# Two-layer hybrid diffusion backbone: three sums of the first layer's conditioning matrix are formed in another stage, four row tiles at a time

## The chip, the core and the metric

The kernel runs on one core of a Trainium2 chip. The metric is the device time of one execution in microseconds; the times before are three runs with a median of 1243.5 us. All other numbers come from one profiled execution of the kernel before. TensorE is written PE, VectorE DVE, ScalarE ACT, GpSimd POOL, and SP is the engine whose queue issues most DMAs.

## The reference, cut to what matters

There are two layers. The first one is attention beside a Fourier mix, both fed by one input projection and joined by one output projection; then a gated convolution FFN. Each layer takes six vectors (two shifts, two scales, two gates) from the conditioning vector c:

```python
def ada_params(cond, w_ada_i, b_ada_i):
    m = jax.nn.silu(cond) @ w_ada_i + b_ada_i          # (1024,) @ (1024, 6*1024)
    ...
    return jnp.split(m, 6, axis=-1)

sh1, sc1, g1, sh2, sc2, g2 = ada_params(c, w_ada[i], b_ada[i])
h_lat = modulate(rmsnorm(x_lat, g_mix[i]), sh1, sc1)
o_lat, o_ctx = hybrid_mixer(h_lat, h_ctx, w_in_hyb[j], ...)     # attention | Fourier, then @ w_out
x_lat = x_lat + g1 * o_lat
h = modulate(rmsnorm(x_lat, g_ffn[i]), sh2, sc2)
x_lat = x_lat + g2 * conv_ffn(h, w_up[i], w_fdw[i], b_fdw[i], w_down[i])
```

The change concerns three of these sums in the first layer: g1 (number 2), sh2 (number 3) and sc2 (number 4). g1 is needed when the output projection is added to x, sh2 and sc2 when the input of the FFN is formed behind it.

## The kernel before

The sequence has 512 rows, so four row blocks of 128. A product in the accurate format is three matmuls of 128x512 (mm3, lines 223 to 225), since each operand is split into a high part (a cast on ACT) and a low part (a subtraction on DVE). Weights arrive as chunks of 512 KB in tiles `st`, are split into `whi` (ACT, L195) and `wlo` (DVE, L196), and five chunks are held at a time.

The mixer runs in this order: input projection of q and kv; then `heads_and_fourier` (projection of the Fourier columns `project(t)`, normalised and rotated heads `k_T`, `q_T`, the transform over time `over_time(t)` with the table `dft`, the transform over channels `over_channels(ct)` with the table `cs`); then `attention`; then `token_major("wo")`, the output projection in two halves.

One sum of w_ada is formed from eight row tiles (`kt`) of 128x1024. For each of them there are two matmuls with cT (128x32) as weights and 512 columns (L338), which write 32 of the 128 rows of one PSUM bank each; the row tile's number, even or odd, and the column half choose which 32, so that two successive row tiles fill four different strips of the array. The trace shows each such fp32 matmul as two records, hence four records for one row tile. `columns` then copies the bank (L344), transposes it in four pieces (L347) and adds strips (L352, L353); `col` adds the bias (L360). `in_every_row` makes the gate a row for all partitions (eight matmuls, L369, and two copies, L370).

Sums 2 and 3 are a filler of `heads_and_fourier`: `fill` stands between its steps, and takes two row tiles at a time from the shared tiles `sa`, of which there are three. Sum 4 is a filler of the output projection: its eight row tiles are loaded into eight tiles `wn` of the pool `xs`, which is opened behind the attention.

Attention works on eight units (a row block and one of two kv heads), with four heads in a unit. For each head there are scores (four matmuls into one of two wide PSUM tiles `D`, L807), a maximum (DVE, L809), an exponential (ACT, L812), a reciprocal (DVE, L814) and a product (POOL, L815). For each unit there are six times four transposes (L824) into a bank `B`, a split of that bank into `pt` (ACT L290, DVE L291) and two matmuls with the values (L829). The scores of a unit are written ahead of the values of the unit before. There are four banks `B`.

The order on each engine is fixed when the program is built, by a scheduler that moves independent instructions past each other by its own estimate of times; every engine then works its list in that order, and the SP queue its own.

Of the kernel before, what the change touches and what calls it, by code (L numbers as in the profile page):

```python
# [17 lines left out]
P = 128  # L18
D = 1024
# [209 lines left out]
def tile_hybrid_backbone(ctx: ExitStack, tc: tile.TileContext, x_in, ctx_in, vecs_in, gains_in, cond_in, condT_in, wada, wnat,  # L229
# [40 lines left out]
    def pad(pool, nbytes):  # L270

        t = pool.tile([P, nbytes // 4], F32, tag="pad", name=nm("pad"), bufs=1)
        nc.gpsimd.memset(t, 0.0)

    pad(const, 32)
    pad(tp, 64)

    def vec(name, i=0, n=1):
        o = VEC[name] + i
        return vecs[:, o : o + n]  # L280
# [31 lines left out]
    def chunk_tile():  # L312
        return wp.tile([P, D], F32, tag="sa", name=nm("sa"), bufs=3)

    class Columns:
# [4 lines left out]
        def __init__(self, pool, row, nbuf):  # L320
            self.pool, self.row, self.nbuf = pool, row, nbuf
            self.st, self.g = [], None

        def load(self, n):
            for _ in range(n):
                if self.pool is None:
                    t = chunk_tile()
                else:
                    t = self.pool.tile([P, D], F32, tag="wn", name=nm("wn"), bufs=self.nbuf)
                nc.sync.dma_start(t, wnat[self.row + len(self.st)])  # L330
                self.st.append(t)
# [21 lines left out]
                nc.vector.tensor_tensor(out=raw[:, s], in0=v[:, s, :, 1, 0:2], in1=part[:, s], op=ALU.add)  # L353
            return raw

        def col(self, j):

            raw = self.columns()
            col = tiny(8)
            nc.vector.tensor_tensor(out=col.rearrange("p (s k) -> p s k", s=2), in0=raw[:, :, :, 0],  # L360
                                    in1=vec("ba", j * KT, KT).rearrange("p (s k) -> p s k", s=2), op=ALU.add)
# [49 lines left out]
    def run(gen, n=1):  # L411
        for _ in range(n):
            if next(gen, "end") == "end":
                return

    def drain(gen):
        for _ in gen:
            pass
# [229 lines left out]
    def heads_and_fourier(q_ps, kv_ps, rot, kgain, qT, kk, vv, four, sums):  # L648
        dft = [four.tile([P, TT, SEQ], F32R, tag=f"dft{i}", name=f"dft{i}") for i in range(2)]
        cs = four.tile([P, 2, 2, P], F32R, tag="cs", name="cs")  # L650
        for i in range(2):
# [92 lines left out]
            nc.vector.tensor_tensor(out=o[:, 257:512][:, ::-1], in0=X[:, 1:256], in1=ys[:, 1:256], op=ALU.add)  # L744
            split(*hsl(h, 4 + ct, 0, SEQ), o)

        def fills():
            for j, use in sums:
                group = Columns(None, j * KT, 0)
                group.load(3)  # L750
                for kt in range(KT):
                    if kt % 2 == 0:
                        yield
                    group.product(kt)
                    if kt + 3 < KT:
                        group.load(1)
                yield
                use(group.col(j))

        filler = fills()  # L760

        def fill():
            run(filler)

        project(0)
        kl = k_rows(0, TT)
        kc = k_rows(TT, NKEY)
# [6 lines left out]
        project(2)  # L774
        q_T(qr, 1)
        qr = [q_rows(2), q_rows(3)]
        fill()
        over_time(0)
        fill()
        over_time(1)  # L780
        fill()
        project(3)
        fill()
        q_T(qr[0], 2)
        q_T(qr[1], 3)
        fill()
        over_time(2)
        fill()
        over_time(3)
        fill()  # L790
        for ct in range(4):
            over_channels(ct)
            fill()
        drain(filler)
    
    def attention(qT, kk, vv, ap, fill):
        units = [(t, kv) for t in range(TT) for kv in range(NKV)]
# [51 lines left out]
    def token_major(key, kts, gate, fin, filler, n_fill):  # L849

        def part(t, kt, w, acc, n):
            mm3(nc, acc, hsl(h, kt, t * P, (t + 1) * P), tuple(u[:, (kt % 2) * 512 : (kt % 2 + 1) * 512] for u in w), n == 0, n == len(kts) - 1)

        D0, D1 = bank2(), bank2()
        acc = [D0[:, 0:512], D0[:, 512:1024], D1[:, 0:512], D1[:, 512:1024]]
        for n, kt in enumerate(kts):
            w = stream.get((key, 0, kt // 2))
            for t in range(TT):
                part(t, kt, w, acc[t], n)
            if n % 2 == 1:  # L860
                stream.release((key, 0, kt // 2))
            run(filler, n_fill)
        drain(filler)
        for t in range(TT):
            residual(t, 0, acc[t], gate)
        for t in range(TT):
            b = bank()
            for n, kt in enumerate(kts):
                part(t, kt, stream.get((key, 1, kt // 2)), b, n)
            residual(t, 1, b, gate)  # L870
            if t == TT - 1:
                for kt in kts[1::2]:
                    stream.release((key, 1, kt // 2))
            fin(t)

    def mixer():
        A2, S2 = mods[0]
        with ExitStack() as tables:
            keep = tables.enter_context(sbuf("keep", "right"))
            gain = keep.tile([P, 2, HD], F32, tag="gain", name="gain")  # L880
            with sbuf("pre") as pre:
                q_ps, kv_ps, rot = load_and_project(gain, keep, pre)
            with sbuf("qkv") as qkv:
                qT = qkv.tile([P, NQ, SEQ], F32R, tag="qT", name="qT")
                kk = [qkv.tile([P, NKV, SEQ + CTX], F32R, tag=f"kk{i}", name=f"kk{i}") for i in range(2)]
                vv = qkv.tile([P, NKEY, NKV, 2, HD], F32R, tag="vv", name="vv")
                with sbuf("four") as four:
                    heads_and_fourier(q_ps, kv_ps, rot, gain[:, 1, :], qT, kk, vv, four, [(2, lambda col: in_every_row(col, gate1)), (3, lambda col: in_rows(col, S2))])
                tables.close()
                with sbuf("att") as ap:  # L890
                    ahead = iter((0, 0, 1, 1, 1, 1, 1, 0))
                    attention(qT, kk, vv, ap, lambda: stream.fill(stream.loaded + next(ahead)))
        with sbuf("xs") as xp:
            group = Columns(xp, 4 * KT, KT)
            group.load(KT)

            def steps():
                for kt in range(KT):
                    yield
                    group.product(kt)  # L900
                in_rows(group.col(4), A2, "gf0")

            token_major("wo", (4, 5, 6, 7, 0, 1, 2, 3), gate1, finisher(xp, A2, S2), steps(), 1)


    def ffn(l, filler, filler1, mods, out_dram=None):
# [382 lines left out]
```

## Time and profile before

| | us |
|---|---|
| median of 3 runs | 1243.5 |
| lowest, highest | 1242.24, 1245.1 |
| the profiled execution's own time | 1242.08 |
| its span, first to last instruction | 1240.3 |
| PE busy in the span | 1172.2 (95%) |
| DVE busy | 764.1 (62%) |
| ACT busy | 588.1 (47%) |
| POOL busy | 260.3 (21%) |
| mean granted PE clock | 0.981 |

The profile's stages are read from the instructions' lines: the Fourier part runs to about 143 us, the attention to about 244 us (with parts of the output projection in its last 27 us), the output projection's remaining part to about 280 us, then the FFN begins. Busy shares are averages over stages with different limits; for the change the stretch from 108 to 258 us matters.

### The profile page before, as it was taken

Reading aid. Unit: us, or ns where it says so; the run is one execution under the profiler, and the core shown is the slowest. Engines: PE = TensorE matmul, PEld = TensorE weight load, DVE = VectorE, ACT = ScalarE, POOL = GpSimd, SP = SyncE. Lnnn points to the kernel's source line nnn. Section 1 sums busy time; section 2 is a strip of 40 time slices with the busy share of each in tenths; the row PEclk is TensorE's granted clock in tenths of the full one; section 3 lists DMA queues with packets and bytes.
Section 4 is the critical chain, followed back from the end, with each engine's and each line's share of the span. In section 5 each row is a group of like instructions: output and inputs, shape, how many; then the busy total and the mean of one; then the engine's idle time right before and its main releaser. Section 6 shows DMA issues by size and latency. Waiting matters only on the chain.

```text
span 1240.3 us, 15425 instructions
## 1 busy us (share of the span) xinstructions
PE 1172.2 (95%) x5813; PEld 962.7 (78%) x5813; DVE 764.1 (62%) x1092; ACT 588.1 (47%) x1021; POOL 260.3 (21%) x164
## 2 busy tenths in 40 slices
PE   4899899999996999999999999979999999999998
PEld 1686477769885888888888877868988888888886
DVE  3458599346987667554646675664686545555563
ACT  4454587325766664334444543342574433433441
POOL 2025255001677830000001650000250000000000
PEclk8999999999998999999999998989999999999999
DMA  9534600222666653222234443101264232232230
GB/s 361 219 135 160 204 1 1 99 105 86 244 224 238 228 206 133 100 89 101 86 102 154 156 139 105 55 17 51 86 207 132 85 103 88 99 102 92 95 119 34
DMA packets 43834, 156.43 MB, mean 126 GB/s; under 512 B 5008, under 2 KB 5520, under 8 KB 43504
## 3 DMA queue, kind: packets, MB, share of 16 engines
q1 hardware_dynamic: 42192, 149.51, 34.9%
q0 software_dynamic: 1120, 5.54, 1.3%
q8 instruction: 46, 0.75, 0.2%
q10 hardware_dynamic: 448, 0.39, 0.1%
q14 instruction: 28, 0.23, 0.1%
HBM read 153.33 MB, written 2.10 MB: 125 GB/s over the span
## 4 chain that ended last, share of the span: by engine, by line
PE 73%; DVE 10%; DMA 7%; ACT 4%; issue 3%; POOL 2%; SPq 0%; POOLq 0%; ACTq 0%; DVEq 0%
PE B L223 17%; PE B L224 16%; PE B L225 16%; PE D L223 6%; PE D L224 6%; PE D L225 6%; DVE wlo L196 3%; DMA sa<-in_wada_dram 3%; DMA st<-in_wall_dram 2%; POOL sa L384 2%; PE B L829 2%; PE B L338 1%; DMA wn<-in_wnat_dram 1%; DVE tiny L809 1%; ACT P L812 1%
## 5 line engine op out<-in xcount | busy, mean ns | idle before, releaser
L196 DVE TENSOR_TENSOR wlo<-st,whi 128x1024 fp32r<-128x1024 f32 x174 | 239.2, 1378 | 245.0 <-ACT whi L195 242.0
L223 PE MATMUL B<-h,whi 128*128 128x512 f32 (+1 forms) x880 | 313.8, 370 | 10.9 <-DVE tmp L925 8.8
L224 PE MATMUL B<-h,whi 128*128 128x512 f32 (+1 forms) x880 | 321.8, 369 | 0.0
L225 PE MATMUL B<-h,wlo 128*128 128x512 f32 (+1 forms) x880 | 320.3, 368 | 0.0
L195 ACT CAST whi<-st 128x1024 fp32r<-128x1024 f32 x174 | 182.1, 1049 | 177.2 <-PE B L224 101.7
L223 PEld LDWEIGHTS B<-h,whi 128*128 128x128 f32 x880 | 162.3, 190 | 39.2 <-issue 9.4
L224 PEld LDWEIGHTS B<-h,whi 128*128 128x128 f32 x880 | 167.2, 190 | 26.8
L225 PEld LDWEIGHTS B<-h,wlo 128*128 128x128 f32 x880 | 166.8, 190 | 27.1
L384 POOL TENSOR_TENSOR sa<-sa,scb 128x1024 f32<-128x1024 f32 x56 | 153.9, 2767 | 79.1 <-DMA sa<-in_wada_dram 39.1
L290 ACT CAST g<-g 128x512 fp32r<-128x512 f32 x88 | 54.6, 621 | 153.6 <-DVE g L933 74.4
L287 POOL TENSOR_TENSOR tiny<-tiny,mhalf 128x1 f32<-128x1 f32 (+3 forms) x26 | 21.2, 816 | 462.4 <-DVE tiny L286 461.2
L291 DVE TENSOR_TENSOR g<-g,g 128x512 fp32r<-128x512 f32 x88 | 69.9, 795 | 71.4 <-ACT g L290 71.4
L387 ACT ACTIVATE sa<-sa 128x512 f32<-128x512 f32 x112 | 69.5, 624 | 30.3 <-POOL sa L384 30.1
L224 PE MATMUL D<-wlo,g 128*128 128x512 f32 x176 | 68.5, 389 | 0.0
L225 PE MATMUL D<-whi,g 128*128 128x512 f32 x176 | 68.5, 389 | 0.0
L223 PE MATMUL D<-whi,g 128*128 128x512 f32 x176 | 68.5, 389 | 0.0
L223 PE MATMUL B<-whi,g 128*128 128x512 f32 x176 | 68.5, 389 | 0.0
L224 PE MATMUL B<-wlo,g 128*128 128x512 f32 x176 | 68.5, 389 | 0.0
L225 PE MATMUL B<-whi,g 128*128 128x512 f32 x176 | 67.8, 389 | 0.0
L924 DVE SCALAR_TENSOR_TENSOR tmp<-B,vecs,tmp 128x511 f32<-128x511 f32 x84 | 62.1, 743 | 5.3 <-ACT tmp L923 5.3
L931 ACT ACTIVATE tmp<-tmp 128x512 f32<-128x512 f32 x44 | 27.8, 631 | 77.9 <-DVE tmp L925 77.1
L923 ACT ACTIVATE tmp<-B,vecs 128x512 f32<-128x512 f32 x84 | 64.4, 771 | 0.0
(239 smaller groups left out, 1919.5 us busy)
## 6 DMA issues: line engine op xcount, KB each, us to landing
st<-in_wall_dram SPq DMA_DIRECT2D x174, 512.0 KB, 3.5
sa<-in_wada_dram SPq DMA_DIRECT2D x56, 512.0 KB, 4.4
wn<-in_wnat_dram SPq DMA_DIRECT2D x24, 512.0 KB, 9.3
sa<-in_wnat_dram SPq DMA_DIRECT2D x16, 512.0 KB, 4.8
x<-in_x_dram SPq DMA_DIRECT2D x4, 512.0 KB, 5.2
dft<-in_dft_dram POOLq DMA_DIRECT2D x2, 1024.0 KB, 6.9
out_dram<-x SPq DMA_DIRECT2D x8, 256.0 KB, 2.0
scb<-in_cond_dram SPq DMA_DIRECT2D x3, 512.0 KB, 5.7
```

The source lines that it names most:

```text
L195: nc.scalar.copy(hi, st)
L196: nc.vector.tensor_tensor(out=lo, in0=st, in1=hi, op=ALU.subtract)
L223: nc.tensor.matmul(out, lhsT=lh, rhs=rh, start=start, stop=False)
L224: nc.tensor.matmul(out, lhsT=lh, rhs=rl, start=False, stop=False)
L225: nc.tensor.matmul(out, lhsT=ll, rhs=rh, start=False, stop=stop)
L290: nc.scalar.copy(hi, src)
L291: nc.vector.tensor_tensor(out=lo, in0=src, in1=hi, op=ALU.subtract)
L384: nc.gpsimd.tensor_tensor(out=st, in0=st, in1=cur["c"], op=ALU.mult)
L387: nc.scalar.activation(out=u, in_=u, func=AF.Identity, accum_out=acc[:, 2 * kt + i : 2 * kt + i + 1])
L923: nc.scalar.activation(out=y, in_=b, func=AF.Identity, scale=w[:, 1:2], bias=vec(f"bfdw{l}", i))
L924: nc.vector.scalar_tensor_tensor(out=y[:, 1:SEQ], in0=b[:, 0 : SEQ - 1], scalar=w[:, 0:1], in1=y[:, 1:SEQ], op0=ALU.mult, op1=ALU.add)
L931: nc.scalar.activation(out=sa, in_=ya, func=AF.Silu)
```

## The change

Sums 2, 3 and 4 are formed by a new class `Block` during the attention. One half of a sum is four row tiles: three in the shared tiles `sa` and one in a new tile `sx`. Their eight matmuls stand together (`product`). The first half's bank is copied by ACT into `gs`, the second half's is added to it by DVE. `col` replaces transposes and strip additions by four matmuls with two columns each (`sel2`, which adds the strips). `fill`, which attention calls behind each unit, takes one step: a product and the loads for the next half; behind a second half the column is formed in the step that follows, ahead of the next product. The fillers of the Fourier part and of the output projection are gone. A small unused tile in the constant pool is gone too, and `sel2` is new there.

```diff
+    class Block:
+        def load(self, half):
+            self.st = []
+            for k in range(4):
+                t = chunk_tile() if k < 3 else self.pool.tile([P, D], F32, tag="sx", name=nm("sx"), bufs=1)
+                nc.sync.dma_start(t, wnat[self.j * KT + 4 * half + k])
+                self.st.append(t)
+        def product(self, half):
+            g = bank()
+            for n, k in enumerate((3, 2, 1, 0)):
+                for s in range(2):
+                    o = 32 * (2 * s + k % 2)
+                    nc.tensor.matmul(g[o : o + 32, :], lhsT=cT[:, 4 * half + k, :], rhs=self.st[k][:, s * 512 : s * 512 + 512], start=n < 2, stop=n >= 2)
+            if half == 0:
+                self.gs = self.pool.tile([P, 512], F32, tag="gs", name=nm("gs"), bufs=1)
+                nc.scalar.copy(self.gs, g)
+            else:
+                nc.vector.tensor_tensor(out=self.gs, in0=g, in1=self.gs, op=ALU.add)
+        def col(self):
+            b = bank()
+            for k in range(4):
+                nc.tensor.matmul(b[:, 2 * k : 2 * k + 2], lhsT=self.gs[:, k * P : (k + 1) * P], rhs=sel2, start=True, stop=True)
             col = tiny(8)
...
-        def fills():
-            for j, use in sums:
-                group = Columns(None, j * KT, 0)
-                group.load(3)
...
-        fill()
         over_time(0)
-        fill()
         over_time(1)
-        fill()
         project(3)
-        fill()
         q_T(qr[0], 2)
         q_T(qr[1], 3)
-        fill()
         over_time(2)
-        fill()
         over_time(3)
-        fill()
         for ct in range(4):
             over_channels(ct)
-            fill()
-        drain(filler)
...
+                    def sums():
+                        todo = []
+                        for j, use in uses:
+                            block = Block(j, ap)
+                            todo += [(block, use, 0), (block, use, 1)]
+                        for n, (block, use, half) in enumerate(todo):
+                            if n == 0:
+                                block.load(0)
+                                yield
+                            block.product(half)
+                            if n + 1 < len(todo):
+                                todo[n + 1][0].load(todo[n + 1][2])
+                            if half == 1:
+                                yield
+                                use(block.col())
+                            else:
+                                yield
+                    def fill():
+                        stream.fill(stream.loaded + next(ahead))
+                        run(filler)
+                    attention(qT, kk, vv, ap, fill)
+                    drain(filler)
         with sbuf("xs") as xp:
-            group = Columns(xp, 4 * KT, KT)
-            group.load(KT)
-            def steps():
-                for kt in range(KT):
-                    yield
-                    group.product(kt)
-                in_rows(group.col(4), A2, "gf0")
-            token_major("wo", (4, 5, 6, 7, 0, 1, 2, 3), gate1, finisher(xp, A2, S2), steps(), 1)
+            token_major("wo", (4, 5, 6, 7, 0, 1, 2, 3), gate1, finisher(xp, A2, S2), chain(), 0)
```

The first place is the PE list where the transform over time ends and the transform over channels begins (`cs`; D<-kk,qT are scores of the first unit). Before:

```order
L338 MATMUL B_1031<-sa_1058,cT 32x512 x2
L338 MATMUL B_1031<-sa_1091,cT 32x512 x2
L807 MATMUL D_1302<-kk_762,qT 128x512
...
L347 MATMUL B_1131<-ident,tmp_1129 128x128 x4
L369 MATMUL B_1144<-ident,tiny_1142 128x128 x4
L369 MATMUL B_1150<-ident,tiny_1142 128x128 x4
L338 MATMUL B_1174<-sa_1156,cT 32x512 x2
L338 MATMUL B_1174<-sa_1158,cT 32x512 x2
L223 MATMUL B_1187<-p_1183,cs 128x258
```

The same place in the changed kernel, PE list:

```order
L224 MATMUL D_1012<-dft_769,f_1062 128x512
L225 MATMUL D_1012<-dft_768,f_1063 128x512
L223 MATMUL B_1112<-p_1108,cs 128x258
L223 MATMUL B_1113<-p_1108,cs 128x256
L224 MATMUL B_1112<-p_1109,cs 128x258
L225 MATMUL B_1112<-p_1108,cs 128x258
```

The sum's products, its transposes and the gate's matmuls stood between the two transforms; now the second transform follows the first one directly.

The second place is the PE list of the changed kernel at the end of the values of the second unit, where sum 2 is finished and the first half of sum 3 is multiplied (L810 are scores, L832 values, L388 the column, L399 the gate, L378 a product):

```order
L832 MATMUL B_1468<-pt_1508,vv 128x512
L388 MATMUL B_1548<-sel_89,gs_1262 128x2 x4
L832 MATMUL B_1468<-pt_1518,vv 128x512
...
L832 MATMUL B_1468<-pt_1530,vv 128x512
L399 MATMUL B_1555<-ident,tiny_1553 128x128 x4
L399 MATMUL B_1561<-ident,tiny_1553 128x128 x4
L378 MATMUL B_1567<-sx_1414,cT 32x512 x2
L378 MATMUL B_1567<-sa_1412,cT 32x512 x2
L378 MATMUL B_1567<-sa_1410,cT 32x512 x2
L378 MATMUL B_1567<-sa_1408,cT 32x512 x2
```

Scores and values of the units have new work between them; such a product stands in six of the eight units.

The third place is the PE list behind the last values of the attention (L829 before, L832 now). Before, the last products of the first half of the output projection and then sum 4:

```order
L223 MATMUL D_2356<-whi_1870,h_84 128x512
L224 MATMUL D_2356<-wlo_1871,h_84 128x512
L225 MATMUL D_2356<-whi_1870,h_85 128x512
L338 MATMUL B_2387<-wn_2339,cT 32x512 x2
...
L338 MATMUL B_2387<-wn_2353,cT 32x512 x2
L347 MATMUL B_2496<-ident,tmp_2494 128x128 x4
L223 MATMUL B_2522<-whi_2002,h_86 128x512
```

The same place in the changed kernel, where B_2510 belongs to the second half of the output projection:

```order
L832 MATMUL B_2297<-pt_2358,vv 128x512
L225 MATMUL B_2510<-whi_2402,h_85 128x512
L832 MATMUL B_2297<-pt_2359,vv 128x512
L223 MATMUL B_2510<-whi_2402,h_84 128x512
L224 MATMUL B_2510<-wlo_2403,h_84 128x512
L225 MATMUL B_2510<-whi_2402,h_85 128x512
L223 MATMUL B_2510<-whi_2432,h_82 128x512
```

Sum 4 is gone from there, and 28 matmuls of the second half stand between the last values and the first product that needs them.

## Rows read from the trace of the kernel before

**Rows 1.** Page: busy time by engine; shares of the chain that ended last

```profile
PE 1172.2 (95%) x5813; PEld 962.7 (78%) x5813; DVE 764.1 (62%) x1092; ACT 588.1 (47%) x1021; POOL 260.3 (21%) x164
...
PE 73%; DVE 10%; DMA 7%; ACT 4%; issue 3%; POOL 2%; SPq 0%; POOLq 0%; ACTq 0%; DVEq 0%
```

**Rows 2.** Sources, line 338: count, duration min/median/max in ns, first and last start

```profile
L338 PE MATMUL B<-sa,cT x64: 592/593/617, 108.1 to 145.5; 128*32 128x512 f32 x64
```

**Rows 3.** Timeline of PE, Fourier part: start, duration in us, instruction [idle before]

```profile
108.10 1.91 PE L338 MATMUL B<-sa,cT 128*32 128x512 f32 x12
109.94 0.51 PE L223 MATMUL B<-whi,h 128*128 128x512 f32 x1
...
119.49 1.05 PE L338 MATMUL B<-sa,cT 128*32 128x512 f32 x4
120.47 0.50 PE L223 MATMUL D<-dft,f 128*128 128x512 f32 x1
...
129.78 2.02 PE L369 MATMUL B<-ident,tiny 128*128 128x128 f32 x16 [1.38 <-DVE tiny L360]
131.73 1.07 PE L338 MATMUL B<-sa,cT 128*32 128x512 f32 x8
132.73 0.39 PE L223 MATMUL B<-p,cs 128*128 128x258 f32 x1
```

**Rows 4.** Timeline of ACT and DVE, from the transforms to the first exponential

```profile
122.13 1.23 DVE L196 TENSOR_TENSOR wlo<-st,whi 128x1024 fp32r<-128x1024 f32 x1
...
124.24 0.59 ACT L290 CAST p<-D 128x512 fp32r<-128x512 f32 x1 [2.03 <-PE D L225]
124.86 0.69 DVE L291 TENSOR_TENSOR p<-D,p 128x512 fp32r<-128x512 f32 x1 [0.79 <-ACT p L290]
...
135.40 0.42 DVE L743 TENSOR_TENSOR tmp<-B,tmp 128x255 f32<-128x255 f32 x1 [5.76 <-ACT tmp L742]
...
141.85 1.28 ACT L812 ACT_TABLE_LOAD   x1
...
143.15 0.90 ACT L812 ACTIVATE P<-D,tiny 128x768 f32<-128x768 f32 x1
```

**Rows 5.** Windows of five attention units, 162.23 to 210.82: sum and mean of one

```profile
sum 48.59, PE 44.90 PEld 35.99 DVE 44.83 ACT 39.08 POOL 29.27; mean PE 8.98 PEld 7.20 DVE 8.97 ACT 7.82 POOL 5.85
```

**Rows 6.** Lines, 171.95 to 210.82 (four units): busy us, mean ns, idle before, releaser

```profile
L824 PE MATMUL B<-ident,P 128*128 128x128 f32 x96 | 15.3, 275 | 1.9 <-POOL P L815 1.9
L809 DVE TENSOR_REDUCE tiny<-D 128x1 f32<-128x768 f32 x16 | 15.2, 951 | 0.0
```

**Rows 7.** Timeline of PE from the last values to the second half

```profile
243.11 1.07 PE L829 MATMUL B<-pt,vv 128*128 128x512 f32 x4
...
246.17 0.50 PE L223 MATMUL D<-whi,h 128*128 128x512 f32 x1 [1.99 <-ACT h L290]
...
249.72 4.11 PE L338 MATMUL B<-wn,cT 128*32 128x512 f32 x24
...
257.48 0.48 PE L223 MATMUL B<-whi,h 128*128 128x512 f32 x1
```

**Rows 8.** Chain that ended last, 243 to 258: start, us, what

```profile
247.13 8.15 DMA wn<-in_wnat_dram
...
257.72 0.23 PE B L223
```

**Rows 9.** Windows: busy us by engine, granted PE clock, DMA share, GB/s

```profile
151.00:153.00 2.00, 1.80 (x6) 1.16 (x5) 1.79 (x5) 0.97 (x5) 1.47 (x1) 0.58 0.00 0
...
247.00:248.00 1.00, 1.00 (x4) 0.78 (x3) 0.00 (x0) 0.00 (x0) 0.00 (x0) 0.50 1.01 414
```

**Rows 10.** Timeline of PE, two groups of scores of the first units

```profile
149.09 0.97 PE L807 MATMUL D<-kk,qT 128*128 128x512 f32 x4
...
151.16 1.54 PE L807 MATMUL D<-kk,qT 128*128 128x512 f32 x4
```

**Rows 11.** Page: DMA issues, KB each, median us to landing

```profile
sa<-in_wnat_dram SPq DMA_DIRECT2D x16, 512.0 KB, 4.8
```

More of the change, by code (lines that the diff above doesn't have):

```diff
@@ L273, in pad @@
         nc.gpsimd.memset(t, 0.0)
-    pad(const, 32)
     pad(tp, 64)
@@ L354, in columns, with __init__ @@
             return raw
-        def col(self, j):
-            raw = self.columns()
+    sel2 = const.tile([P, 2], F32, tag="sel2", name="sel2")
+    nc.vector.tensor_tensor(out=sel2, in0=ident[:, 0:P:64], in1=ident[:, 32:P:64], op=ALU.add)
+    class Block:
+        def __init__(self, j, pool):
+            self.j, self.pool = j, pool
+        def load(self, half):
[19 more added lines that the diff above has]
+                nc.tensor.matmul(b[:, 2 * k : 2 * k + 2], lhsT=self.gs[:, k * P : (k + 1) * P], rhs=sel2, start=True, stop=True)
             col = tiny(8)
-            nc.vector.tensor_tensor(out=col.rearrange("p (s k) -> p s k", s=2), in0=raw[:, :, :, 0],
-                                    in1=vec("ba", j * KT, KT).rearrange("p (s k) -> p s k", s=2), op=ALU.add)
+            nc.vector.tensor_tensor(out=col.rearrange("p (s k) -> p k s", s=2), in0=b[:, 0:8].rearrange("p (k s) -> p k s", s=2),
+                                    in1=vec("ba", self.j * KT, KT).rearrange("p (s k) -> p k s", s=2), op=ALU.add)
             return col
@@ L646, in rotary, with heads_and_fourier @@
         eng.tensor_tensor(out=d3, in0=d3, in1=r[:, :nh].unsqueeze(2).to_broadcast([P, nh, HD]), op=ALU.mult)
-    def heads_and_fourier(q_ps, kv_ps, rot, kgain, qT, kk, vv, four, sums):
+    def heads_and_fourier(q_ps, kv_ps, rot, kgain, qT, kk, vv, four):
         dft = [four.tile([P, TT, SEQ], F32R, tag=f"dft{i}", name=f"dft{i}") for i in range(2)]
@@ L745, in over_channels @@
             split(*hsl(h, 4 + ct, 0, SEQ), o)
-        def fills():
-            for j, use in sums:
-                group = Columns(None, j * KT, 0)
-                group.load(3)
-                for kt in range(KT):
-                    if kt % 2 == 0:
-                        yield
-                    group.product(kt)
[L755 to L763, printed above, removed]
         project(0)
@@ L887, in mixer @@
                 with sbuf("four") as four:
-                    heads_and_fourier(q_ps, kv_ps, rot, gain[:, 1, :], qT, kk, vv, four, [(2, lambda col: in_every_row(col, gate1)), (3, lambda col: in_rows(col, S2))])
+                    heads_and_fourier(q_ps, kv_ps, rot, gain[:, 1, :], qT, kk, vv, four)
                 tables.close()
@@ L891, in mixer @@
                     ahead = iter((0, 0, 1, 1, 1, 1, 1, 0))
-                    attention(qT, kk, vv, ap, lambda: stream.fill(stream.loaded + next(ahead)))
-        with sbuf("xs") as xp:
-            group = Columns(xp, 4 * KT, KT)
-            group.load(KT)
-            def steps():
-                for kt in range(KT):
-                    yield
-                    group.product(kt)
-                in_rows(group.col(4), A2, "gf0")
-            token_major("wo", (4, 5, 6, 7, 0, 1, 2, 3), gate1, finisher(xp, A2, S2), steps(), 1)
+                    uses = ((2, lambda col: in_every_row(col, gate1)), (3, lambda col: in_rows(col, S2)), (4, lambda col: in_rows(col, A2, "gf0")))
+                    def sums():
[15 more added lines that the diff above has]
+                                yield
+                    filler = sums()
+                    run(filler)
+                    def fill():
+                        stream.fill(stream.loaded + next(ahead))
+                        run(filler)
+                    attention(qT, kk, vv, ap, fill)
+                    drain(filler)
+        with sbuf("xs") as xp:
+            token_major("wo", (4, 5, 6, 7, 0, 1, 2, 3), gate1, finisher(xp, A2, S2), chain(), 0)
     def ffn(l, filler, filler1, mods, out_dram=None):
```

## The prediction, made before the changed kernel ran

> **What bounds the kernel now.** I read the page first: PE is busy 95% of the span and holds 73% of the chain that ended last [rows 1]. So whatever stands on PE's list costs its length, unless it fills a hole there. The second view was the line of the moved work: 64 records of sum products in the Fourier part [rows 2], more behind the attention (24 of them in one piece [rows 7]). Then the timelines, stage by stage, since a moved product costs different things in the three places.
>
> In the Fourier part PE waits little, but the products themselves are badly packed. A row tile alone (x4 records) takes 0.98 us from its start to the start of the next matmul, 119.49 to 120.47; two row tiles together (x8) take 1.00, 131.73 to 132.73 [rows 3]. So a second row tile is nearly free when it stands right beside the first, and nine of the sixteen stand alone.
>
> In the attention PE and DVE are busy alike, 8.98 and 8.97 of 9.72 us in a unit [rows 5]; 0.74 us of PE is idle, of which 1.9/4 = 0.48 is the first transposes' wait for POOL [rows 6]. Nothing there has much room.
>
> Behind the attention PE does useful work for 2.1 us only (nine matmuls at 0.23 [rows 8]) between the end of the last values, 243.11 + 1.07 = 244.18, and the second half of the output projection at 257.48 [rows 7]. The rest is a hole of 1.99 us, half speed, and sum 4 with a transfer of 8.15 us in the chain [rows 8].
>
> **The change, part by part.**
>
> *Fourier part, a gain.* PE loses the three adjacent row tiles at 108.10 (1.84 us until 109.94 [rows 3]) and three single ones at 0.98, all ahead of the split of the first transform's result, `p`. By PE alone p would come 1.84 + 2.94 = 4.8 us sooner. But on ACT and DVE two weight chunks are split ahead of p, and the last of these subtractions ends only at 122.13 + 1.23 = 123.36 [rows 4]; it hangs on a load whose start follows earlier weight work, and moves by 1.84 at most. I put it at 122.2 (I take 1.2 of the 1.84), so p's first subtraction ends at 122.2 + 0.69 = 122.9, where it was 125.55: 2.65 sooner. From there to the first exponential it took 143.15 - 125.55 = 17.6 us, with products, transposes, a wait of 1.38 and the gate's 2.02 between the transforms. In the new order only the DVE and ACT chain is left. DVE in the order of its list: p 0.69, two combinations 0.84, p 0.69, h 0.69, the first maximum 0.95 [rows 6], combinations 0.84, p 0.69, combinations 0.84, together 6.2; then ACT: one cast 0.59, two small copies for which I put 0.5, the table load 1.28 [rows 4]. 122.9 + 6.2 + 2.4 = 131.5 against 143.15, 11.6 us sooner. The first of the six products falls into the first unit's scores, where PE waits for exponentials anyway, and costs nothing; if that cover were gone it would cost 2.0.
>
> PE is then half idle from about 121 to 133, and its clock can fall. The trace shows this: at 151 to 153 the granted clock is 0.58, most of the time the lower of the two levels (1.2 instead of 2.4 GHz), after a stretch in which PE waited in every group of scores, and these take 1.54 us instead of 0.97 [rows 9, 10]; behind the hole of 1.99 us it is 0.50 [rows 7, 9]. A first product at half speed is 2.0 us longer, four groups of scores 4 x 0.57 = 2.3: 4.3 at worst, 0 at best, and I take 1.5, since part of the chain is DVE's. Gain 10; bounds 7.3 (all of the low clock) and 13.8 (none, and no weight split in the way).
>
> The Trainium skill speaks against the change here: in "TensorE: Matmul & The Clock Gate", section "Loop structure matters more than you think", matmuls that follow each other keep the clock up and waits between them let it fall. By that rule the old fillers earned something, for the clock read 1.00 while they stood there, and taking them out would cost the whole 4.3; by the rows the same fillers also cost more than that in length.
>
> *Attention, a cost.* Five products stand in the steady units, two passes of 1.00 each: 5 x 2.0 = 10. The gate's matmuls bring their 2.02 along. The column is new: four fp32 matmuls, eight records; at the gate's price of 2.02/16 per record 1.0 each, three of them 3.0 (from 0.3 each, since they have two columns only, to the gate's whole 2.0 each). Together 15. Off goes what fills a hole: the wait for POOL is the one that a product ahead of the next unit's transposes can cover, and I take 0.4 in each of five units, 2.0. Cost 13; bounds 12 + 0.9 - 7 x 0.74 = 7.7 and 12 + 6 = 18. DVE gets three additions of half a row and three tiny ones, ACT three copies and the gate's two; beside PE's 2 us per unit they are hidden, and would cost about 0.7 each if DVE became the bound.
>
> Its loads: the four of one half are issued when the product before has read the tiles, behind it on SP only loads that come later anyway. One lands in 4.8 us [rows 11], the last of eight at once in 8.15 [rows 8]; products lie a unit, 9.7 us or more, apart. I cost them at nothing. The first `sx` has to wait for the table's memory and for SP's two weight loads ahead, until about 123, and lands at about 128, five ahead of its use.
>
> *Behind the attention, a gain.* Between 244.18 and 257.48 lie 13.3 us, of which 2.1 are needed. 7.76 belong to sum 4 and its transposes (249.72 to 257.48) and surely go; the hole of 1.99 and about 1.5 of half speed go if something fills the hole, and in the new list 28 matmuls, 28 x 0.23 = 6.4 us, stand between the last values and the first product that needs them. Gain 10, bounds 7.8 and 11.2. What is late next is PE itself: behind 257.48 its list is full.
>
> *The rest.* `sel2` is one tiny operation at the start; the removed small tile costs nothing. Later stages I take as shifted.
>
> Sum: -10 + 13 - 10 = -7. The profiled execution took 1242.08 us (span 1240.3), 1.4 below the median of 1243.5, so this gives 1235.1 for it and, against the median, 1236.5; I say 1236.
>
> **Rivals.**
>
> *The attention swallows more.* If every unit gives its whole 0.74 and the columns cost 0.3, the cost is 7.7 instead of 13: 1236 - 5 = 1231. For it: DVE gets 2 us per unit to run ahead. Against: a hole is only filled by a product that happens to stand at it, and six of them stand in eight units.
>
> *Given back.* The clock falls for the whole of the first unit (gain 7.3), the attention fills no hole (cost 15), and the hole behind it stays (gain 7.8): -0.1, so 1243.5, no change. For it: equal load of PE and DVE, so that a stop of one becomes a stop of the other. The rule on the clock from the page named above would do its part of this.
>
> *Banks, and slower.* Four banks B serve the attention: one gathers a unit's values, three carry the transposes. Six products, three columns and the gate's two halves take one each, eleven times. If each time PE must wait until ACT and DVE have emptied a bank, 0.59 + 0.69 = 1.28 us, this is 14 us more: 1236 + 14 = 1250. It becomes slower from 0.9 us each (a gain of 7 to be eaten, and 2.5 beyond). For it: in the second unit column, gate and product come together. Against: in the steady units PE waits for no bank now, and behind a product ACT and DVE have had 2 us to empty.
>
> *It does not happen as written.* The first product waits for its load, and PE behind it: it has five us to spare, and only a queue that runs 10 us late makes it cost 5, 1241.
>
> **How the numbers follow.** Forecast 0.60, attention swallows more 0.15, given back 0.13, banks 0.09, late load 0.03. A difference below 0.2% (2.5 us) cannot be told from none. Faster than 1241: the first two, and a little of the others, 0.77; within 0.2%: 0.14; slower: 0.09. The corners of the bounds are 1226 and 1246; the range of 1229 to 1244 holds the forecast with its unknown column and clock, the first rival, the second and the late load, and leaves out the banks and the ends of the others.
>
> **What would show it.** Right: the first exponential at 130 to 134; no single row tile in the Fourier part; attention units with a product 11.0 to 11.7 us long, the one with the gate about 14; less than 1 us between the last values and the output projection, and no transfer in its chain. Wrong: waits of PE for ACT or DVE behind each product (banks), a granted clock of 0.5 beyond the first unit, or products that wait for DMA.

## The result

The changed kernel takes 1225.64 us (median of four runs, 1222.35 to 1229.67) against 1243.7 in the same session: a ratio of 0.9856, 95% interval 0.9823 to 0.9890. Run again as e5 it took 1224.88 and 0.9853 (0.9834 to 0.9873). It is faster, as forecast, but by 18 us instead of 7.5, and outside the range of 1229 to 1244.

### The profile page after: what moved, and what is told of

Same layout as the page of the kernel before. It is cut to its first block, busy times and chain, and to the rows that moved or that the text cites. A ratio compares the mean times of both kernels' runs of the same rounds, so it can differ in the third digit from the quotient of the medians.

```text
span 1225.2 us, 15441 instructions
## 1 busy us (share of the span) xinstructions
PE 1165.5 (95%) x5825; PEld 963.0 (79%) x5825; DVE 768.3 (63%) x1090; ACT 587.4 (48%) x1015; POOL 259.5 (21%) x163
## 4 chain that ended last, share of the span: by engine, by line
PE 78%; DVE 10%; DMA 5%; ACT 3%; issue 2%; POOL 1%; SPq 0%; ACTq 0%; DVEq 0%; POOLq 0%
PE B L223 18%; PE B L224 17%; PE B L225 17%; PE D L223 6%; PE D L224 6%; PE D L225 6%; DVE wlo L196 3%; DMA st<-in_wall_dram 3%; PE B L832 2%; ACT whi L195 1%; PE B L827 1%; PE D L810 1%; PE B L378 1%; POOL sa L414 1%; DMA wn<-in_wnat_dram 1%
## 5 line engine op out<-in xcount | busy, mean ns | idle before, releaser
L195 ACT CAST whi<-st 128x1024 fp32r<-128x1024 f32 x174 | 182.0, 1049 | 169.6 <-PE B L224 99.2
L224 PEld LDWEIGHTS B<-h,whi 128*128 128x128 f32 x880 | 166.5, 189 | 27.1 <-DVE h L481 0.2
L225 PE MATMUL B<-whi,g 128*128 128x512 f32 x176 | 67.8, 389 | 0.0
```

Source lines behind the costliest of these rows:

```text
L195: nc.scalar.copy(hi, st)
L224: nc.tensor.matmul(out, lhsT=lh, rhs=rl, start=False, stop=False)
L225: nc.tensor.matmul(out, lhsT=ll, rhs=rh, start=False, stop=stop)
```

## The profile after

The page of the changed kernel, profiled at 1227.01 us: PE busy and the chain's shares by engine, as in [rows 1].

```profile
PE 1165.5 (95%) x5825; PEld 963.0 (79%) x5825; DVE 768.3 (63%) x1090; ACT 587.4 (48%) x1015; POOL 259.5 (21%) x163
PE 78%; DVE 10%; DMA 5%; ACT 3%; issue 2%; POOL 1%; SPq 0%; ACTq 0%; DVEq 0%; POOLq 0%
```

PE is busy 6.7 us less; the rest is idle time that went. To compare stages, two instructions serve that every kernel here has in the same order: the casts of the weight chunks on ACT (L195, 174 of them). The eleventh stands ahead of the Fourier part, the 31st in the FFN, behind all that the change touches. The timelines of ACT at these two, start in us, for before, for the changed kernel, and for before once more (e9); here and below, lines of one block need not be neighbours in the view:

```profile
85.72 1.05 ACT L195 CAST whi<-st 128x1024 fp32r<-128x1024 f32 x1 [1.28 <-PE B L225]
339.85 1.04 ACT L195 CAST whi<-st 128x1024 fp32r<-128x1024 f32 x1
```

```profile
89.50 1.05 ACT L195 CAST whi<-st 128x1024 fp32r<-128x1024 f32 x1 [1.28 <-PE B L225]
329.82 1.04 ACT L195 CAST whi<-st 128x1024 fp32r<-128x1024 f32 x1
```

```profile
89.08 1.05 ACT L195 CAST whi<-st 128x1024 fp32r<-128x1024 f32 x1 [1.28 <-PE B L225]
342.95 1.04 ACT L195 CAST whi<-st 128x1024 fp32r<-128x1024 f32 x1
```

The stretch between them is 254.13 and 253.87 us in the two traces of before, and 240.33, 240.89 and 240.68 in three of the changed kernel (e5 and e8 with it): 13.4 us less, repeatable to half a microsecond. What lies ahead of the eleventh cast (85.6 to 89.5 us over all traces) and behind the 31st (894.6 to 900.6) varies by 3.9 and 6.0 us, although the same work is done there; the forecast of the gain was 7.5. From here on a place in a trace is given as its distance from the eleventh cast; for exponentials these are the starts of L812 before and L815 after.

| from the eleventh cast to, us | before, e9 | changed, e5, e8 | e1, no sums |
|---|---|---|---|
| first subtraction of p | 39.14, 39.17 | 34.74, 34.62, 34.77 | 34.68 |
| first exponential | 57.43, 57.44 | 44.07, 43.94, 44.09 | 44.01 |
| 4th exponential | 64.40, 64.41 | 52.09, 51.20, 52.00 | 50.38 |
| 32nd exponential | 132.50, 132.23 | 127.49, 127.82, 127.40 | 118.22 |
| 31st cast | 254.13, 253.87 | 240.33, 240.89, 240.68 | 228.76 |

*Fourier part.* DVE and ACT in the changed kernel, answering to [rows 4]:

```profile
122.98 1.22 DVE L196 TENSOR_TENSOR wlo<-st,whi 128x1024 fp32r<-128x1024 f32 x1
124.24 0.69 DVE L290 TENSOR_TENSOR p<-D,p 128x512 fp32r<-128x512 f32 x1
132.27 1.28 ACT L815 ACT_TABLE_LOAD   x1
133.57 0.90 ACT L815 ACTIVATE P<-D,tiny 128x768 f32<-128x768 f32 x1
```

From p's subtraction to the first exponential it is 9.33 us (18.29 before). The last weight subtraction starts 33.48 us from the eleventh cast instead of 36.41, so 2.93 sooner. Before, p did not wait for it but for PE: ACT stood idle for 2.03 us until the transform's matmuls ended [rows 4]. Now ACT's cast of p starts 33.52 us from the eleventh cast instead of 38.52, and p follows the weight subtraction at once. The load of the last weight chunk ahead of p, in three views: of the two weight loads issued between 113 and 119 us before, the time to landing; in the chains of the changed kernel and of e10 (below; there its subtraction comes behind the first p), the load's start and length:

```profile
DMA to landing us min/median/max: 4.3/4.8/5.2
117.77 4.11 DMA st<-in_wall_dram
115.67 6.91 DMA st<-in_wall_dram
```

Before, it was issued at 115.38 us and its cast started at 120.56, so it is the one of 5.2 us. From the eleventh cast it is issued 1.39 us sooner in the changed kernel, its cast follows 1.05 sooner after that, and the subtraction 0.49 sooner after the cast: together the 2.93. Then PE in the first unit:

```profile
134.61 1.65 PE L810 MATMUL D<-kk,qT 128*128 128x512 f32 x4 [2.57 <-ACT P L815]
137.06 2.54 PE L378 MATMUL B<-sa,cT 128*32 128x512 f32 x10
```

```profile
132.50:139.00 6.50, 4.39 (x20) 1.76 (x20) 4.16 (x9) 4.53 (x8) 2.93 (x2) 0.50 0.00 1
```

Here, behind a chain that is DVE's and a wait of 2.57 us for the exponential, PE runs at the lower level (second view, a window: length, busy time of PE, PEld, DVE, ACT, POOL, granted clock 0.50, share and rate of DMA). Scores take 1.65 us; before, a group took 1.54 a unit later, at a granted clock of 0.58 [rows 9, 10].

*Attention.* A product and a column in the changed kernel's units:

```profile
151.44 0.62 PE L378 MATMUL B<-sx,cT 128*32 128x512 f32 x2
153.30 0.96 PE L832 MATMUL B<-pt,vv 128*128 128x512 f32 x3
162.51 0.95 PE L388 MATMUL B<-sel,gs 128*128 128x2 f32 x8
163.32 0.96 PE L832 MATMUL B<-pt,vv 128*128 128x512 f32 x3
165.04 1.95 PE L399 MATMUL B<-ident,tiny 128*128 128x128 f32 x16
166.91 0.62 PE L378 MATMUL B<-sx,cT 128*32 128x512 f32 x2
```

From start to the next start: a product 1.86, a column 0.81, the gate 1.87. Five products, three columns and one gate are 13.6 us. The windows from the 8th to the 32nd exponential (columns as above) of before and of the changed kernel:

```profile
159.90:218.22 58.32, 53.90 (x313) 43.17 (x312) 53.73 (x102) 46.92 (x97) 35.00 (x25) 1.00 0.00 1
```

```profile
151.10:216.99 65.89, 64.80 (x418) 47.73 (x417) 54.87 (x107) 47.90 (x99) 34.72 (x25) 1.00 0.40 152
```

PE had 4.42 us of idle time in these six units and has 1.09 now; the wait for POOL of [rows 6], 3.8 us in eight times between 150 and 219 us before, is 0.8 in one. These are all waits of PE in the changed kernel between 141 and 217 us (total, times, longest):

```profile
PE D L810 <- ACT P L815: 1.1, 1, 1.1
PE B L832 <- DVE pt L290: 0.9, 3, 0.4
PE B L827 <- POOL P L818: 0.8, 1, 0.8
```

*Behind the attention.* PE at the end of the values, answering to [rows 7, 8]:

```profile
246.59 0.39 PE L225 MATMUL B<-whi,h 128*128 128x512 f32 x1
246.82 0.39 PE L832 MATMUL B<-pt,vv 128*128 128x512 f32 x1
247.05 0.39 PE L223 MATMUL B<-whi,h 128*128 128x512 f32 x1
```

Hole, transfer and transposes are gone: the next product starts 0.23 us behind the last value.

## The experiments

Times are medians beside before in the same session; "stretch" is eleventh to 31st cast, 254.0 before and 240.6 changed. Median and stretch need not agree: behind the 31st cast e1, e3 and e10 take 899.8 to 900.6 us and the changed kernel 895.3 to 897.0, although they differ from it only ahead of that cast.

**e1, no sums at all.** The filler is not run, gate and rows are set by `memset(…, 0.01)`:

```diff
-                    run(filler)
+                    nc.vector.memset(gate1, 0.01)   # and S2, A2
-                        run(filler)                # in fill()
-                    drain(filler)
```

> This is the changed kernel without the three sums in the attention: gate, shift and scale of the FFN are set to a constant by three small writes instead (left out: the 24 row tiles, their loads, columns and the gate's matmuls). Changed kernel 1225.6 us. What leaves PE's list: six products, three columns of 0.81 and a gate of 1.87 us, five products at 1.86 us in the steady units: 13.6 us, and a first one that ran at half clock. Theory H (holes): the units' idle time took 4 to 5 us of it, so its price is about 9, and 1 more for the first product: 1215 to 1217; the fourth to the 32nd exponential take 66 to 67 us instead of 75.4. Rival P (prediction's price, 13 us): 1211 to 1213, and 62.4 between the exponentials. Rival F (the work in the attention is free and what was gained came from elsewhere): 1222 to 1225, and 73 or more.

1217.97 us, ratio 0.9798 (0.9768 to 0.9828), 7.7 us faster than the changed kernel; stretch 228.76, 11.9 us shorter.

```profile
149.10:207.38 58.28, 53.82 (x313) 43.09 (x312) 53.77 (x103) 46.86 (x97) 35.10 (x25) 1.00 0.00 1
```

The same six units are as long as before (58.28 and 58.32). So the sums cost 7.6 us there, 0.8 to 1.7 ahead of the 4th exponential (the first product, over three traces of the changed kernel), and 2.3 to 2.7 behind the 32nd, where PE has 16 matmuls and 2.3 us of work more than in e1, pushed out of the six units. By the stretch that is between P and H: about 10.2 us for 13.6 of work, 3.4 in holes. By H's own numbers it is just beside it: 67.8 us between the 4th and the 32nd exponential, and a median 1 us above H's range. The first exponential comes as in the changed kernel (44.01), so all of the gain up to there is from taking the sums, matmuls and loads together, away.

**e2, each product twice.**

```diff
-            for n, k in enumerate((3, 2, 1, 0)):
+            for n, k in 2 * tuple(enumerate((3, 2, 1, 0))):
```

> This is the changed kernel with each of the six products in the attention computed twice, the second time over the first. Added: 6 times 1.86 = 11.2 us of PE work at the places of the products. Theory H (holes): the units have 3.0 us of idle PE left in 75.4, and a longer product reaches the same hole, so nearly all of it shows: plus 9 to 11, 1235 to 1237, units with a product 1.7 to 1.9 us longer each. Rival P (the prediction's full price, two per product): plus 12, 1238. Rival F (there is free room yet in each unit): plus 0 to 6, 1226 to 1232.

1243.39 us, ratio 1.0013 (0.9994 to 1.0033): 18 us on the changed kernel, more than any theory said; stretch 256.98, 16.3 more. A part is that the order changed too: PE at one of the doubled products,

```profile
184.58 1.44 PE L378 MATMUL B<-sa,cT 128*32 128x512 f32 x6
185.95 0.50 PE L832 MATMUL B<-pt,vv 128*128 128x512 f32 x1
186.38 1.05 PE L378 MATMUL B<-sa,cT 128*32 128x512 f32 x4
187.36 0.50 PE L832 MATMUL B<-pt,vv 128*128 128x512 f32 x1
```

where the last row tile stands alone and takes 0.98 us. It shows that no room is left (F is out), but not the price of one product.

**e3, sum 4 stays.** The third entry of `uses` is dropped, and before's loads, `steps()` and `n_fill` 1 are put back.

> This is the changed kernel with sums 2 and 3 alone in the attention; sum 4 stays beside the output projection as in the kernel before (eight tiles loaded behind the attention, products, transposes). Theory: the part behind the attention is worth about 9 us (hole 1.99, half clock 1.5, 7.8 of sum 4 and its transposes, less what fills nothing), and sum 4 costs 2 x 1.86 + 0.81 = 4.5 in the attention, of which 1 to 2 fell into holes: the kernel is 5 to 7 us slower than the changed one, 1231 to 1233, and the hole of 2 us with the wait for the transfer is back. Rival: what stood behind the attention was hidden by the projection's other limits (weight splits); then leaving sum 4 there costs nothing and saves its 3 us in the attention: 1222 to 1224.

1235.57 us, ratio 0.9941 (0.9926 to 0.9957); stretch 248.51, 7.9 longer. PE behind the attention:

```profile
241.81 0.50 PE L223 MATMUL D<-whi,h 128*128 128x512 f32 x1 [1.54 <-ACT h L289]
244.09 2.09 PE L337 MATMUL B<-wn,cT 128*32 128x512 f32 x8
246.38 1.05 PE L337 MATMUL B<-wn,cT 128*32 128x512 f32 x4 [0.20 <-DMA wn<-in_wnat_dram]
254.73 0.48 PE L223 MATMUL B<-whi,h 128*128 128x512 f32 x1
```

The hole is back (1.54), and sum 4 takes 10.6 us, six of its row tiles alone and each waiting for its transfer; in the kernel before it took 7.8 [rows 7], so e3 makes the place look dearer than it was. The difference is more than the 5 to 7 expected; the rival is out.

**e4, pairs in the Fourier part.** The kernel before, with

```diff
-                    group.product(kt)
-                    if kt + 3 < KT:
-                        group.load(1)
+                    group.product(kt + 1)      # for kt in 0, 2, 4, 6
+                    group.product(kt)
+                    group.load(max(0, min(2, KT - kt - 3)))
```

> This is the kernel before with one edit: in the Fourier part the second row tile of each pair is written first, so that all sixteen row tiles of sums 2 and 3 stand in adjacent pairs instead of nine alone. Place, columns and sum 4 are as before. Nothing is moved to another stage. Theory (place): nine single row tiles become pairs, which saves about 9 x 0.98 / 2 = 4.4 us of PE, of which some 3 count on the chain to the first exponential: it comes about 3 us sooner, time 1239 to 1242 against 1243.7. Rival (packing): the gain in the Fourier part of the change, 12 us up to the fourth exponential, is one of packing; then this edit has most of it, 1232 to 1236, with the first exponential at 133 to 136.

1246.29 us, ratio 1.0035 (1.0017 to 1.0053), slower; stretch 260.00. All sixteen stand in pairs, and PE shows what this brings with it:

```profile
129.18 1.94 PE L338 MATMUL B<-sa,cT 128*32 128x512 f32 x8 [2.75 <-DMA sa<-in_wnat_dram]
134.11 3.75 PE L369 MATMUL B<-ident,tiny 128*128 128x128 f32 x16 [1.15 <-DVE tiny L360]
```

p came 1.8 us sooner (37.31), but a pair waits for two loads in three tiles, and PE, waiting, fell to half speed with the gate (3.75 us, 2.02 in [rows 3]) between the transforms. The theory was wrong in size and sign, and so was the rival: at the old place and with three tiles, pairs do not bring the gain of the Fourier part. What packing is worth without those waits, this run does not show.

**e5, the changed kernel again.**

> This is the changed kernel itself, run again for a narrow interval and for a second trace. In the first traces everything up to the weight split at 340 us gives a gain of 13.8 us against before once the different start is taken off, and behind it another 5.0 us, in a stage in which both run the same instructions. Theory C (the rest is where the stretches at half clock happen to fall): the gain by many runs is 14 to 16 us, 1227 to 1229, and the stage behind 340 us differs from that of the first trace by some us. Rival (the later stages are truly shorter): 18 us or more, 1225 or less, and the later stage repeats to within 1 us.

1224.88 us; stretch 240.89, behind it 897.0 us (895.4 in the first trace, 900.5 before). The median says rival, the traces say C for a part: see below.

**e6, the first product in the Fourier part's last hole.** Three row tiles go into `sa`, the fourth into two free `qs` tiles, issued behind `q_rows(3)`; `block.product(0)` stands behind `over_channels(3)`.

> This is the changed kernel with its first product moved once more: its four row tiles are loaded into tiles that are free from 108 us on, and it stands in the hole of 1.2 us in which PE waits for the split of the last p of the Fourier part (130.60 in the changed kernel's trace); all later pieces come one unit sooner. Theory (holes): the first product cost about 1.7 us between the first and the fourth exponential (136.19 to 139.53, at half clock), and this goes; as the later pieces find the same holes, 1 to 3 us faster than the changed kernel. Rival (the product stands in the transforms' chain, as the old fillers did): the first exponential comes 0.6 to 2 us later and the kernel is no faster, 0 to 2 us slower.

1224.88 us, ratio 0.9852 (0.9832 to 0.9873): no faster than the changed kernel. Stretch 238.25, 2.4 less, so theory by the trace, not settled by times.

```profile
129.95 0.62 PE L389 MATMUL B<-two,cT 128*32 128x512 f32 x2 [0.67 <-issue]
131.81 0.39 PE L224 MATMUL B<-p,cs 128*128 128x258 f32 x1
```

The product takes 1.86 at full speed instead of 3.3 (136.19 to 139.53 in the changed kernel), and the first exponential comes 0.8 later (44.87).

**e7, another order of the four.** `enumerate((3, 1, 2, 0))`, start and stop by n % 2.

> This is the changed kernel with another order of the four row tiles of a product (3, 1, 2, 0 for 3, 2, 1, 0), so that two row tiles that follow each other write the same strips of the array and only the middle two can run beside each other: three passes of 0.43 x 2 = 0.86 us for two. Nothing else changes, neither loads nor results. Added: six times 0.86 = 5.2 us of PE. Theory (holes are full): all of it shows, 4 to 6 us slower than the changed kernel. Rival (packing is what makes the change pay; without it each row tile takes a pass of its own): six times 1.7, 10 us slower. Rival (there is room): 0 to 2 us.

1227.38 us, ratio 0.9874 (0.9854 to 0.9895); stretch 242.01.

```profile
151.34 0.62 PE L378 MATMUL B<-sx,cT 128*32 128x512 f32 x2
153.21 0.97 PE L832 MATMUL B<-pt,vv 128*128 128x512 f32 x3
```

The product takes 1.87, as before: writing the same strips twice running costs PE nothing here. So this run added no work and says nothing on the price; my picture of the strips was wrong. The 1.4 us that the stretch is longer arise behind the 32nd exponential, where nothing was changed.

**e8, padding.** `pad(const, 32)` put back.

> This is the changed kernel with the small unused tile of 32 bytes that the change removed put back, which shifts the addresses of what is allocated behind it. Theory: it costs and gives nothing, within 2 us of the changed kernel, with the same times of the first and the 32nd exponential. Rival (the shifted addresses are part of the gain): 3 us or more slower than the changed kernel, in every stage alike.

1224.74 us, ratio 0.9855 (0.9830 to 0.9880); stretch 240.68. The theory holds: the addresses play no part that these times could show.

**e9, the kernel before again.**

> This is the kernel before, for a second trace. Three traces with the changed kernel's Fourier part and attention (changed, again, padded) gain 13.3 to 13.8 us by the weight split at 340 us, their start taken off, yet the median of runs gains 18 to 18.7. Theory C (the rest is where the stretches at half clock fall, in the start and behind 340 us, and the first trace of before drew few in the start): this trace is 1 to 4 us later than the first at 85 us, and differs from it behind 340 us by 1 to 4 us. Rival (one piece of the gain lies where both run the same instructions, as a lasting effect): it repeats the first trace of before within 1 us in both stretches.

1241.27 us, ratio 0.9995 (0.9975 to 1.0015). The start is 3.4 us longer than in the first trace, the stage behind the 31st cast 2.2 shorter, the stretch the same: theory C holds for the traces. One piece does repeat, as the rival said: from the 96th to the 102nd cast it is 29.0 and 29.2 us in the two traces of before, and 27.0 to 27.1 in three of the changed kernel.

**e10, the loads alone.** At the old places of `fill` two loads each, without products:

```diff
+            for u in held:
+                nc.gpsimd.tensor_tensor(out=tiny(8), in0=u[:, 0:8], in1=mhalf, op=ALU.mult)
+            held.clear()
+            for _ in range(2):
+                held.append(chunk_tile())
+                nc.sync.dma_start(held[-1], wnat[2 * KT + next(count)])
```

> This is the changed kernel with 16 loads of 512 KB put back into the Fourier part, into the three shared tiles and at the places where the kernel before loaded the row tiles of sums 2 and 3; a small GpSimd operation reads each, and its result is not used. PE gets nothing. Changed kernel 1224.9 us; first subtraction of p at 120.46 and first exponential at 129.75, both less the later start of 3.78 us at 85 us of its trace (before: 124.86 and 143.15). Theory Q (the old loads stood in SP's queue ahead of the last weight chunks, and by that held up the weight split which stands ahead of p): p comes 1 to 2.5 us later, the first exponential as much, the kernel 1226 to 1228. Rival PE (the matmuls alone held p up): both as in the changed kernel within 0.5 us.

1234.95 us, ratio 0.9952 (0.9932 to 0.9973): 10 slower than the changed kernel without one more matmul; stretch 246.97, 6.3 more. SP's queue, ACT and DVE:

```profile
109.83 4.77 SPq L787 DMA_DIRECT2D sa<-in_wnat_dram  x4
114.70 0.38 SPq L194 DMA_DIRECT2D st<-in_wall_dram  x1
116.14 6.64 SPq L787 DMA_DIRECT2D sa<-in_wnat_dram  x3
120.06 1.04 ACT L195 CAST whi<-st 128x1024 fp32r<-128x1024 f32 x1 [3.16 <-DMA st<-in_wall_dram]
121.14 1.22 DVE L196 TENSOR_TENSOR wlo<-st,whi 128x1024 fp32r<-128x1024 f32 x1 [3.50 <-ACT whi L195]
122.39 0.69 DVE L290 TENSOR_TENSOR p<-D,p 128x512 fp32r<-128x512 f32 x1
```

Loads of sums stand ahead of weight loads, ACT waits 3.16 us for a chunk, and p comes at 36.80 instead of 34.74: 2.06 later, as much as Q said. The first exponential is 3.7 later (47.75), more than Q said, and the first product slips behind the 4th exponential. The first two products are broken up (the row tile in `sx` at 140.26, its three others at 147.66; then 153.57 and 156.59), and by the 32nd exponential the kernel is 6.2 behind.

This shows what loads ahead of weight chunks can do, but not that they did it in the kernel before. The loads stand otherwise here: the cast that waits 3.16 us starts 34.47 us from the eleventh cast, where it stood at 32.63 before with a wait of 0.45 us for its chunk, and no wait for a load is in the chain to p of the kernel before. Whether the queue's order or the shared transfer bandwidth holds the chunk was not separated.

**e11, sum 4 on POOL and ACT.** `ada_rows(0, 4, A2, "gf0")` behind two sums.

> This is the changed kernel with the last of the three sums taken off PE in the attention: its eight row tiles are multiplied on POOL with the conditioning vector in every row and added up on ACT (two halves each), as the kernel does for later sums in the FFN. PE loses two products and a column, 2 x 1.86 + 0.81 = 4.5 us; POOL gets eight products of 128x1024, ACT sixteen half rows, one SiLU and two table loads of 1.28 us. Theory (PE bounds the attention; POOL with 34.7 busy of 65.9 us and ACT with 47.9 have room): 2 to 4 us faster than the changed kernel, 1221 to 1223. Rival (POOL's product stands between each exponential and the transposes; a row tile in front of it makes PE wait): 3 to 12 us slower, 1228 to 1237, with waits of PE for POOL.

1235.62 us, ratio 0.9952 (0.9933 to 0.9971), 10 slower; stretch 246.53, 5.9 more. The rival is right in sign and size, not in mechanism. In the attention,

```profile
L414 POOL TENSOR_TENSOR sa<-sa,sx 128x1024 f32<-128x1024 f32 x8 | 19.3, 2420 | 2.6 <-ACT tmp L834 2.6
L417 ACT ACTIVATE sa<-sa 128x512 f32<-128x512 f32 x16 | 10.1, 644 | 0.0
```

```profile
PE D L810 <- ACT P L815: 6.1, 6, 1.3
PE B L827 <- POOL P L818: 0.8, 1, 0.8
```

(the second view: waits, as above). A POOL product of a row tile lasts 2.42 us, but PE's growing wait is for ACT's exponentials, 6.1 us for 1.1, not for POOL, 0.8 as in the changed kernel. ACT has 10.1 us of half rows in its list there; that these hold up the exponentials is argued, not shown.

## Why the prediction was wrong

**The Fourier step failed.** It said that the last weight subtraction "moves by 1.84 at most", and took 1.2: only the matmuls removed ahead of its load were counted. It moved 2.93, of which 1.39 are the load's earlier issue, 1.05 its faster landing and 0.49 less work of DVE behind its cast; so p came 4.40 us sooner, not 2.65. That this subtraction, and no longer PE, would set p was right. The landing was taken as given: with no loads of row tiles in flight the chunk lands in 4.1 us, with before's in 5.2, with e10's ahead of it in 6.9. That the loads of the sums make this difference is likely; e10 does not measure their share in the kernel before. The rest of the chain came out: 8.6 us from p's end to the first exponential, 8.64 measured. That it agrees so closely is in part luck, since the chain in the trace also runs over PE. So the first exponential came 13.4 sooner, not 11.6 (at 129.8 us, reckoned from before's eleventh cast, just ahead of the 130 to 134 named as a sign). The low clock cost less than the 1.5 taken: between the first and the fourth exponential the gain shrinks by 0.3 to 1.1 us in three traces. The first product, costed at nothing, has a price of 0.8 to 1.7 there (e1). At the 4th exponential the gain is 12.3 to 13.2 instead of 10.

**The attention term was too large.** Work 13.6 instead of 15 (a product 1.86 for 2.0, a column 0.81 for 1.0), and 3.4 us in holes instead of 2.0: 10.2 by e1, for 13. The reading that POOL's wait is what a product covers was right; but it covers nearly all of it, while I took 0.4 in five units. Units with a product last 10.4 to 11.6 us (11.0 to 11.7 expected), and the one with the gate 10.7, not 14. The rival "swallows more" had the direction.

**Behind the attention** the mechanism held. From the 32nd exponential to the 31st cast the changed kernel gains 8.5 us, with about 2.6 us of the attention's work paid there (e1): 11.1, about the upper bound (11.2), for 10. The output projection did fill the hole.

Together: -12.3 + 10.2 - 11.1 = -13.2 against -7; the stretch says -13.4. All three sizes lay inside their bounds and erred to one side. With this gain alone the time would be 1230.3 us, inside the range: that it fell outside takes the part below as well, which the prediction put at nothing ("Later stages I take as shifted"). "Given back" and "banks" did not come: there is no wait for a bank in the attention's rows, and the low clock ends with the first unit. The granted clock is 0.50 at 132.5 to 139 and 1.00 at 139.5 to 149.5; before, it read 0.58 at 151 to 153, in the second unit [rows 9], so little was lost. By the Trainium skill (TensorE: Matmul & The Clock Gate, "Loop structure matters more than you think") waits between matmuls let the clock fall. The trace agrees in kind.

**Later stages were not just shifted, and why is open.** The medians differ by 18 us, the stretch by 13.4. On average over two traces of before and three of the changed kernel, the start is 0.9 us longer in the changed kernel and the part behind the 31st cast 3.4 shorter. Of these 3.4, 2.0 lie between the 96th and the 102nd cast, where PE waits and its clock falls: granted clock 0.55, 0.50 and 0.82 in three windows of 3 us from 755.19 us before, 0.67 and 0.76 in two from 742.37 us in the changed kernel. But e1 and e10, which differ from the changed kernel only far ahead of it, take 28.8 and 28.6 us there, and e2 27.0, so no run ties this piece to the moved sums. About 2 us remain on which traces and medians may simply have drawn differently; before itself runs from 1235.6 to 1246.7.

## What to carry to other kernels

When a filler is moved, price its loads where they stood in the queue as well as its matmuls: a chunk loaded among them landed 2.8 us later in e10, and in the kernel before, probably for that reason, 1 us. Work put into a stage that is nearly full on PE costs its length less the holes, and removing it is the clean way to measure that; doubling it changed the order and measured something else. When several terms of a sum have one-sided bounds, let the range reach to the corners, and leave room for stages that the change does not touch: the corner here was 1226, still above the measured time.

## What the runs showed of the hardware

Two row tiles that write the same two strips one behind the other took as long as two that fill four (1.87 and 1.86 us for four, e7 and changed kernel). A row tile alone still takes 0.98 [rows 3], so it is adjacency that pays, whatever the strips. And the start up to the eleventh cast, 85.7 and 89.1 us long in two traces of one kernel, shows how little a difference of 3 us says without a common mark.
